# Where the operands begin in SBUF: moving operands of 256 columns 192 bytes (modulo 256) beyond the stationary ones

## The chip, the cores and the metric

The kernel runs on one core of one Trainium2 chip. The metric is device time in microseconds, the median of several executions. A profiled execution gives the trace that is read below; TensorE's granted clock in it is 0.999 of 2.4 GHz.

## What is computed

One decoder layer on 512 tokens of width 1024, in float32:

```python
x = x + 0.5 * swiglu(rms_norm(x, n1), gate1, up1, down1)        # d_ff = 2816
z, xbc, dt, q, k, v = split(rms_norm(x, nm) @ w_in)             # width 5648
y_ssd = gated_norm(ssd_chunked(conv(xbc), dt, ...), silu(z))    # Mamba-2, 4 chunks of 128
o = diff_attention(q_norm(q), k_norm(k), v)                     # 8 heads, causal
x = x + concat(y_ssd, o) @ w_out
x = x + 0.5 * swiglu(rms_norm(x, n2), gate2, up2, down2)
```

## The kernel before

All large products run on TensorE in three terms: an operand is split into a high part of type fp32r and the rest, and hi·hi, hi·lo and lo·hi are added up in PSUM. Weights arrive by DMA from SyncE's queue as `raw` pieces of 128x1024; ScalarE casts them into `whi` (L112), VectorE subtracts to get `wlo` (L113). Both are rings of four buffers, each 4096 bytes per partition.

Each matmul has a weight load of its own: TensorE first reads the stationary operand (128 columns, 512 bytes per partition), then streams the moving one past it. There are three families:

- **256 columns in the two FFNs.** All of gate and up except the first part goes through a product of 2x2 blocks that takes seven block products in place of eight (`seven`). Its innermost lines, L310 to L312, have a weight block as stationary operand and 256 columns of prepared activations (`ah`, `al`) as the moving one:

```python
for i in range(4):
    hi, lo = (z[:, off + i * P:off + (i + 1) * P] for z in w)
    PE.matmul(ps, lhsT=hi, rhs=ah[:, i, a], start=i == 0, stop=False)
    PE.matmul(ps, lhsT=hi, rhs=al[:, i, a], start=False, stop=False)
    PE.matmul(ps, lhsT=lo, rhs=ah[:, i, a], start=False, stop=i == 3)
```

- **256 columns in the mixer's projections** z, v and q|k (`tok_proj`, L597 to L599). Here the activations `xhm`, `xlm` are stationary and 256 columns of `whi` or `wlo` move.
- **512 columns** (`mm3`, L154 to L156): the first part of gate and up (`gu`), `xbc`, the down products (`dn`) and the output projection (`wo`). A weight block is stationary; 512 columns of activations move (`xh`, `xl`, `xhm`, `xlm`, `h`, `yh`, `yl`, or the attention's `ov`, `ool`).

Smaller products in plain fp32 (attention, the SSD chunks, transposes) and the narrow dt projection (`psdt`, L491 to L495) stand between them.

Tiles come from pools that are laid out one behind the other in each partition's SBUF, so the sizes of the tiles ahead decide where a tile begins. Four tiles that nothing reads or writes are there already (`padc`, `padr`, `padt`, `pads`), and two tiles are made wider than they are used (`row`, `u`). With these, every large operand of a matmul begins at a multiple of 256 bytes. The pools that the change touches are `xn` (the normalised activations `xh`, `xl`, `xhm`, `xlm`, later `yh`, `yl`, and two scratch tiles of `seven`), `str1` and `str2` (`ah` and `al` of each FFN) and `mix` (with `row`).

A scheduler orders the instructions when the program is built; waits are on semaphores that it sets.

Of the kernel before, what the change touches and what calls it, by code (L numbers as in the profile page):

```python
# [8 lines left out]
F32 = mybir.dt.float32  # L9
# [9 lines left out]
P = 128  # L19
# [15 lines left out]
NROW = 1456  # L35
# [3 lines left out]
def hymba_layer(ctx: ExitStack, tc: tile.TileContext, xT, gu1, dn1, wxbc, wdt, wz, wv, wqk,  # L39
# [148 lines left out]
    tiny.tile([P, 8], F32, tag="padt", name="padt", bufs=1)  # L188
    xn_cm = tc.tile_pool(name="xn", bufs=1)
    xnpool = xn_cm.__enter__()  # L190

    def rsqrt(dst, v, shape, tag):

        y = tiny.tile(shape, F32, tag=f"rs_y{tag}", name="rs_y")
        t = tiny.tile(shape, F32, tag=f"rs_t{tag}", name="rs_t")
        ti = t.bitcast(I32)
        V.tensor_scalar(ti, v.bitcast(I32), 1, None, op0=ALU.arith_shift_right)
        V.tensor_scalar(y.bitcast(I32), ti, -1, 0x5F3759DF, op0=ALU.mult, op1=ALU.add)
        for it in range(3):
            V.tensor_mul(t, y, y)  # L200
            V.scalar_tensor_tensor(t, t, -0.5, v, op0=ALU.mult, op1=ALU.mult)
            V.scalar_tensor_tensor(dst if it == 2 else y, t, 1.5, y, op0=ALU.add, op1=ALU.mult)
# [68 lines left out]
    def ffn(xn, x, done, name, parts, early):  # L271
# [6 lines left out]
        sp_cm = tc.tile_pool(name=f"str{name}", bufs=1)  # L278
        hp_cm = tc.tile_pool(name=f"ffn{name}", bufs=5)
        sp, hp = sp_cm.__enter__(), hp_cm.__enter__()  # L280
        ah = sp.tile([P, 4, 7, 256], F32R, name=f"ah{name}")
        al = sp.tile([P, 4, 7, 256], F32R, name=f"al{name}")

        def operands(i):

            tx = hp.tile([P, 8, 256], F32, tag="hp", name="tx")
            for k, at in ((i, 6), (i + 4, 0)):
                c = xn.wcol + k
                V.scalar_tensor_tensor(tx[:, at:at + 2, :].rearrange("p a b -> p (a b)"), x[k], col[:, c:c + 1],
                                       xn.rbc, op0=ALU.mult, op1=ALU.mult)  # L290
            V.tensor_add(tx[:, 2], tx[:, 7], tx[:, 1])
            V.tensor_sub(tx[:, 3], tx[:, 2], tx[:, 6])
            V.tensor_sub(tx[:, 4], tx[:, 6], tx[:, 7])
            V.tensor_sub(tx[:, 5], tx[:, 0], tx[:, 3])
            S.copy(ah[:, i], tx[:, 0:7])
            V.tensor_sub(al[:, i], tx[:, 0:7], ah[:, i].bitcast(F32))
# [102 lines left out]
    def done1(d):  # L399
# [3 lines left out]
        G.dma_start(xsave[d], x1[d])  # L403

    ffn(n1, x1, done1, "1", PARTS1, EARLY1)
    nm = nm[0]
    xpool_cm.__exit__(None, None, None)
# [1 line left out]

    mix_cm = tc.tile_pool(name="mix", bufs=1)  # L410
    mix = mix_cm.__enter__()
    row = mix.tile([P, 1536], F32, name="row")[:, :NROW]
    nc.sync.dma_start(row, rows.partition_broadcast(P))
    vt = [mix.tile([P, NB, 256], F32, tag=f"v{g}", name=f"v{g}") for g in range(4)]

# [597 lines left out]
    def done2(d):  # L1013
        nc.sync.dma_start(out[d], x2[d])

    ffn(n2, x2, done2, "2", PARTS2, EARLY2)


# [59 lines left out]
```

## Time and profile before

| | us |
|---|---|
| median of 3 runs | 1167.11 (1165.74 to 1168.05) |
| the profiled execution | 1164.7 |
| its span, first to last instruction | 1163.0 |
| TensorE busy (matmuls) | 1153.9, 99% |
| TensorE weight loads | 1029.2, 89% |
| VectorE busy | 854.4, 73% |
| ScalarE busy | 545.8, 47% |

A matmul's record in the trace is longer than the time that it holds TensorE back: the next one starts while it still drains. What counts for the time is the distance from one start to the next. "PEld" are the weight loads, which run while the matmul ahead streams.

### The profile page before, as it was taken

The numbers are of one execution on the slowest core, as the hardware profiler recorded it, in microseconds if no ns is written. First come the engines' busy times: TensorE is split into PE (matmuls) and PEld (weight loads), VectorE is DVE, ScalarE is ACT, GpSimd is POOL, SyncE is SP. The second block draws the span as 40 slices with busy tenths as digits, with TensorE's granted clock in tenths as the row PEclk, the third lists the DMA queues.
The fourth block names the chain that finished last, engine by engine and source line by source line (L and its number), as shares of the span: only waits on it lengthen the run. The fifth ranks groups of instructions, "written<-read, shape, count | busy, mean of one in ns | idle before, by whom it ended". The sixth has DMA issues, their size and how long they took to land.

```text
span 1163.0 us, 18640 instructions
## 1 busy us (share of the span) xinstructions
PE 1153.9 (99%) x7435; PEld 1029.2 (89%) x7435; DVE 854.4 (73%) x1509; ACT 545.8 (47%) x938; POOL 37.2 (3%) x63
## 2 busy tenths in 40 slices
PE   8999999999999999999999999999999999999998
PEld 6889999999988789999988887788889999999997
DVE  6987877887758976685387877535798888787763
ACT  5443333433345458883466656434354443334331
POOL 2000000000004000000000000022000000000000
PEclk9999999999999999999999999999999999999999
DMA  7323333333336242343321204154223333333332
GB/s 235 92 69 97 94 102 112 105 100 105 91 115 222 73 146 74 110 126 92 109 74 37 72 21 130 43 172 127 73 64 100 109 114 96 112 102 100 104 106 86
DMA packets 42391, 119.53 MB, mean 103 GB/s; under 512 B 4608, under 2 KB 9920, under 8 KB 42304
## 3 DMA queue, kind: packets, MB, share of 16 engines
q1 hardware_dynamic: 41024, 114.15, 32.2%
q0 software_dynamic: 1280, 4.20, 1.0%
q8 instruction: 58, 0.95, 0.3%
q14 instruction: 29, 0.24, 0.1%
HBM read 112.00 MB, written 6.32 MB: 102 GB/s over the span
## 4 chain that ended last, share of the span: by engine, by line
PE 99%; DMA 0%; DVE 0%; SPq 0%; POOL 0%; issue 0%; ACT 0%
PE s L312 10%; PE s L311 10%; PE s L310 10%; PE dn L155 7%; PE dn L154 7%; PE dn L156 7%; PE gu L154 3%; PE gu L155 3%; PE gu L156 3%; PE qk L597 3%; PE qk L599 3%; PE qk L598 3%; PE wo L154 3%; PE wo L156 3%; PE wo L155 3%; PE sc L820 2%
## 5 line engine op out<-in xcount | busy, mean ns | idle before, releaser
L112 ACT CAST whi<-raw 128x1024 fp32r<-128x1024 f32 (+2 forms) x217 | 189.4, 875 | 314.0 <-PE s L311 125.8
L113 DVE TENSOR_TENSOR wlo<-raw,whi 128x1024 fp32r<-128x1024 f32 (+3 forms) x225 | 223.1, 993 | 124.7 <-ACT whi L112 117.8
L311 PE MATMUL s<-al,whi 128*128 128x256 f32 x952 | 268.4, 283 | 0.0
L310 PE MATMUL s<-ah,whi 128*128 128x256 f32 x952 | 267.1, 283 | 0.0
L312 PE MATMUL s<-ah,wlo 128*128 128x256 f32 x952 | 266.4, 283 | 0.0
L311 PEld LDWEIGHTS s<-al,whi 128*128 128x128 f32 x952 | 182.6, 192 | 1.9
L310 PEld LDWEIGHTS s<-ah,whi 128*128 128x128 f32 x952 | 181.9, 192 | 2.0
L312 PEld LDWEIGHTS s<-ah,wlo 128*128 128x128 f32 x952 | 181.5, 192 | 0.1
L155 PE MATMUL dn<-h,whi 128*128 128x512 f32 x352 | 137.4, 391 | 0.0
L112 ACT CAST whi<-tw 128x1024 fp32r<-128x1024 f32 x68 | 70.4, 1050 | 141.6 <-PE s L311 76.0
L156 PE MATMUL dn<-h,wlo 128*128 128x512 f32 x352 | 136.6, 390 | 0.0
L154 PE MATMUL dn<-h,whi 128*128 128x512 f32 x352 | 136.2, 390 | 0.0
L113 DVE TENSOR_TENSOR wlo<-tw,whi 128x1024 fp32r<-128x1024 f32 x68 | 81.9, 1218 | 3.5 <-ACT whi L112 3.4
L156 PEld LDWEIGHTS dn<-h,wlo 128*128 128x128 f32 x352 | 66.1, 188 | 13.4
L154 PEld LDWEIGHTS dn<-h,whi 128*128 128x128 f32 x352 | 66.2, 188 | 12.9
L155 PEld LDWEIGHTS dn<-h,whi 128*128 128x128 f32 x352 | 66.3, 188 | 12.0
L597 PE MATMUL qk<-whi,xhm 128*128 128x256 f32 x256 | 75.0, 293 | 0.0
L599 PE MATMUL qk<-whi,xlm 128*128 128x256 f32 x256 | 72.8, 284 | 0.0
L598 PE MATMUL qk<-wlo,xhm 128*128 128x256 f32 x256 | 72.4, 283 | 0.0
L346 DVE SCALAR_TENSOR_TENSOR x<-dn,x 128x512 f32<-128x512 f32 x64 | 44.0, 687 | 34.9 <-PE dn L156 33.7
L154 PE MATMUL gu<-xh,whi 128*128 128x512 f32 x160 | 63.9, 400 | 2.3 <-POOL whi L110 2.2
L156 PE MATMUL gu<-xh,wlo 128*128 128x512 f32 x160 | 63.0, 394 | 0.0
(274 smaller groups left out, 2239.8 us busy)
## 6 DMA issues: line engine op xcount, KB each, us to landing
raw<-in_gu SPq DMA_DIRECT2D x86, 512.0 KB, 3.5
raw<-in_dn SPq DMA_DIRECT2D x48, 384.0 KB, 3.1
raw<-in_wqk SPq DMA_DIRECT2D x16, 512.0 KB, 3.6
raw<-in_wxbc SPq DMA_DIRECT2D x12, 512.0 KB, 3.8
raw<-in_wo SPq DMA_DIRECT2D x10, 512.0 KB, 4.2
raw<-in_dn SPq DMA_DIRECT2D x16, 256.0 KB, 2.7
raw<-in_wz SPq DMA_DIRECT2D x8, 512.0 KB, 3.6
ab<-acs_d SPq DMA_DIRECT2D x8, 512.0 KB, 3.8
```

The costliest lines, as they stand in the source:

```text
L112: S.copy(hi[:, a:b], raw[:, a:b])
L113: V.tensor_sub(lo[:, a:b], raw[:, a:b], hi[:, a:b].bitcast(F32))
L154: PE.matmul(ps, lhsT=hi, rhs=xh, start=start, stop=False)
L155: PE.matmul(ps, lhsT=hi, rhs=xl, start=False, stop=False)
L156: PE.matmul(ps, lhsT=lo, rhs=xh, start=False, stop=stop)
L310: PE.matmul(ps, lhsT=hi, rhs=ah[:, i, a], start=i == 0, stop=False)
L311: PE.matmul(ps, lhsT=hi, rhs=al[:, i, a], start=False, stop=False)
L312: PE.matmul(ps, lhsT=lo, rhs=ah[:, i, a], start=False, stop=i == 3)
L346: V.scalar_tensor_tensor(x[d], ps, 0.5, x[d], op0=ALU.mult, op1=ALU.add)
L597: PE.matmul(o, lhsT=xh, rhs=hi, start=k == 0, stop=False)
L598: PE.matmul(o, lhsT=xh, rhs=lo, start=False, stop=False)
L599: PE.matmul(o, lhsT=xl, rhs=hi, start=False, stop=k == KD - 1)
```

## The change

Three unused tiles are added and one tile loses its unused end. The instructions, their order on all five engines, and their waits stay the same; only addresses differ.

```diff
@@ -188,6 +188,7 @@
     xn_cm = tc.tile_pool(name="xn", bufs=1)
     xnpool = xn_cm.__enter__()
+    xnpool.tile([P, 16], F32, name="padx")
@@ -278,8 +279,10 @@
         sp, hp = sp_cm.__enter__(), hp_cm.__enter__()
+        sp.tile([P, 32 if name == "1" else 48], F32, name=f"pada{name}")
         ah = sp.tile([P, 4, 7, 256], F32R, name=f"ah{name}")
         al = sp.tile([P, 4, 7, 256], F32R, name=f"al{name}")
+        sp.tile([P, 16], F32, name=f"padb{name}")
@@ -409,7 +412,7 @@
-    row = mix.tile([P, 1536], F32, name="row")[:, :NROW]
+    row = mix.tile([P, NROW], F32, name="row")
```

What it does to the distance from the start of the stationary operand to the start of the moving one (bytes, modulo 256), from the addresses of the two built programs:

| fp32r matmuls | count | before | after |
|---|---|---|---|
| 256 columns, FFN (L310 to L312) | 2856 | 0 | 192 |
| 256 columns, z, v, q and k (L597 to L599) | 1536 | 0 | 192 |
| 512 columns: gu of the first FFN 288, xbc 288, wo from yh and yl 192 | 768 | 0 | 64 |
| 512 columns: dn 1056, gu of the second FFN 192, wo from the attention 192 | 1440 | 0 | 0 |
| 512 columns, psdt, with 48 or 16 stationary columns | 16 | 0, 64, 128, 192 | 0, 64, 128, 192 |

The plain fp32 products keep their distances. After the change `xh`, `xl`, `xhm`, `xlm`, `yh`, `yl` begin 64 bytes after a multiple of 256 (in the second FFN `xh` and `xl` come from another pool and stay at a multiple), `ah` and `al` 192 bytes after one; the weights stay where they were. In `tok_proj` the activations at 64 are stationary and the weights at 0 move, which makes 192 again.

## Rows read from the trace of the kernel before

**Rows 1.** The page: the span, busy time by engine, granted clock, chain that ended last.

```profile
span 1163.0 us, 18640 instructions
PE 1153.9 (99%) x7435; PEld 1029.2 (89%) x7435; DVE 854.4 (73%) x1509; ACT 545.8 (47%) x938; POOL 37.2 (3%) x63
...
PEclk9999999999999999999999999999999999999999
...
PE 99%; DMA 0%; DVE 0%; SPq 0%; POOL 0%; issue 0%; ACT 0%
PE s L312 10%; PE s L311 10%; PE s L310 10%; PE dn L155 7%; PE dn L154 7%; PE dn L156 7%; PE gu L154 3%; PE gu L155 3%; PE gu L156 3%; PE qk L597 3%; PE qk L599 3%; PE qk L598 3%; PE wo L154 3%; PE wo L156 3%; PE wo L155 3%; PE sc L820 2%
```

**Rows 2.** Groups by line, TensorE: matmuls of 256 columns (count, busy us, mean ns).

```profile
L311 PE MATMUL s<-al,whi 128*128 128x256 f32 x952 | 268.4, 283 | 0.0
...
L597 PE MATMUL qk<-whi,xhm 128*128 128x256 f32 x256 | 75.0, 293 | 0.0
...
L597 PE MATMUL z<-whi,xhm 128*128 128x256 f32 x128 | 39.0, 305 | 0.0
...
L597 PE MATMUL v<-whi,xhm 128*128 128x256 f32 x128 | 38.0, 297 | 0.0
```

**Rows 3.** Timeline, matmuls, a run of 84 of 256 columns (start us, duration us).

```profile
155.19 0.28 PE L310 MATMUL s<-ah,whi 128*128 128x256 f32 x1
...
165.26 0.40 PE L154 MATMUL dn<-h,whi 128*128 128x512 f32 x1
```

**Rows 4.** Timeline, matmuls, the first and the last of 31 of 512 columns.

```profile
351.95 0.39 PE L154 MATMUL dn<-h,whi 128*128 128x512 f32 x1
...
358.75 0.39 PE L156 MATMUL dn<-h,wlo 128*128 128x512 f32 x1
```

**Rows 5.** Timeline, weight loads: 16 in a row, with short matmuls (64 columns).

```profile
454.83 0.19 PEld L599 LDWEIGHTS z<-whi,xlm 128*128 128x128 f32 x1
454.95 1.88 PEld L693 LDWEIGHTS pd<-xdt,ab 128*128 128x128 f32 x16
```

**Rows 6.** Timeline, matmuls: the first of 256 columns behind one of 512.

```profile
136.46 0.28 PE L310 MATMUL s<-ah,whi 128*128 128x256 f32 x1
136.57 0.28 PE L311 MATMUL s<-al,whi 128*128 128x256 f32 x1
136.69 0.28 PE L312 MATMUL s<-ah,wlo 128*128 128x256 f32 x1
```

**Rows 7.** Tile s: count, duration ns min/median/max.

```profile
L310 PEld LDWEIGHTS s<-ah,whi x952: 187/192/192, 77.3 to 1125.6; 128*128 128x128 f32 x191
L310 PE MATMUL s<-ah,whi x952: 274/283/283, 77.5 to 1125.7; 128*128 128x256 f32 x191
```

**Rows 8.** Timeline, matmuls of psdt, the first and the last of 16.

```profile
382.59 0.40 PE L491 MATMUL psdt<-xhm,dtw 128*48 128x512 f32 x1
...
386.04 0.39 PE L491 MATMUL psdt<-xhm,dtw 128*48 128x512 f32 x1
```

**Rows 9.** Timeline, matmuls of 512 columns behind rows 3: the second and the seventh.

```profile
165.50 0.40 PE L155 MATMUL dn<-h,whi 128*128 128x512 f32 x1
...
166.65 0.39 PE L154 MATMUL dn<-h,whi 128*128 128x512 f32 x1
```

**Rows 10.** Timeline, plain fp32: two records of 512 columns, then the next.

```profile
459.73 1.02 PE L675 MATMUL pd<-state,cT 128*128 128x512 f32 x2
460.59 1.02 PE L681 MATMUL st<-xdd,btok 128*128 128x512 f32 x2
```

**Rows 11.** Busy time by stretch: a stretch of seven-products, and one of z and v.

```profile
core 0: us, PE busy (x) PEld busy (x) DVE busy (x) ACT busy (x) POOL busy (x), PEclk, DMA share, GB/s
77.00:170.00 93.00, 93.00 (x646) 87.08 (x645) 74.05 (x112) 36.28 (x44) 0.00 (x0) 1.00 0.35 103
436.00:520.00 84.00, 84.00 (x667) 79.67 (x666) 60.73 (x102) 72.19 (x195) 0.00 (x0) 1.00 0.31 98
```

**Rows 12.** What TensorE waited for longest (us in total, times, longest).

```profile
PE gu L154 <- POOL whi L110: 2.2, 1, 2.2
```

## The prediction

> **What bounds the kernel now.** I read the page first. TensorE is busy 99% of the span, 1153.9 of 1163.0 us, and the chain that ended last is TensorE for 99% as well; the granted clock stands at the upper level, 2.4 GHz, throughout [rows 1]. The longest thing that TensorE waited for by the list of waits is one wait of 2.2 us at the start [rows 12]. So a nanosecond on each matmul is a nanosecond on the time, and the only question is what sets the distance from one matmul to the next. The groups by line say how many there are: 952 at each of L310 to L312, and 256, 128 and 128 at each of L597 to L599 for q and k, z and v [rows 2]. That is 2856 + 1536 = 4392 matmuls of 256 columns. The timeline gives their distance: a run of 84 takes 165.26 − 155.19 = 10.07 us, 119.9 ns each [rows 3]. So these are 4392 × 119.9 ns = 527 us, 45% of the span. For 512 columns, 30 distances fill 358.75 − 351.95 = 6.80 us, 226.7 ns each [rows 4]. The two differ by 106.8 ns for 256 columns, 0.417 ns a column, one column per cycle at 2.4 GHz. What is left over is 13.1 ns with 256 columns and 13.2 ns with 512. With plain fp32, whose 512 columns take 0.86 / 2 = 430 ns a record, that is twice 0.417 ns a column and only 3 ns are left over [rows 10]. A moving operand read at full rate thus costs some 10 ns more than one at half rate, and that is the part which an address could change.
>
> **Two limits under the 119.9.** The first is the weight load. Sixteen loads in a row, behind which only 64 columns stream at a time, last 1.88 us; one alone lasts 0.19, so (1.88 − 0.19) / 15 = 112.7 ns lie between two [rows 5]. The second is the stream itself: 106.8 ns and the 3 ns of the fp32 case make 109.8. The load is the higher floor, so 256 columns can come down to 112.7 at best, 7.2 ns less than now. That the floor is within reach with addresses of this kind is seen once in each run: the first matmul of 256 columns behind one of 512 is followed after 0.11 us, and the next after 0.12 [rows 6]. By the tile's view a record there lasts 274 ns at the least against a median of 283, and a load 187 against 192 [rows 7]. So shape and rate alone do not make 119.9; it is the steady state that two overlapping streams settle into.
>
> **What the change does, part by part.**
>
> *256 columns, 4392 matmuls.* No instruction is added, removed or moved; the moving operand starts 192 bytes beyond the stationary one, modulo 256, instead of at the same residue. The trace of before has no such matmul, so the cost is bounded. The stream moves on by 4 bytes in 0.417 ns, 9.6 bytes per ns, and the load covers 512 bytes in at most 112.7 ns, some 4.5 bytes per ns. If both start together the stream gains about 5 bytes per ns, some 540 in one matmul, twice 256. At offset 0 they then meet at the start, in the middle and again at the end; at any other offset twice. That meetings at the same residue cost time is my reading, not a row. Lower bound: 112.7 ns, a gain of 7.2 × 4392 = 31.6 us. Upper bound: the matmuls of psdt, whose distances modulo 256 run through 0, 64, 128 and 192, take (386.04 − 382.59) / 15 = 230.0 ns each, 3.3 more than 226.7 [rows 4, 8]; on 4392 that is a loss of 14.5 us. The two ends differ in sign. I take 114 ns, close to the 0.11 us of the case that is nearest in shape and rate [rows 6] and a little above the floor: a gain of 5.9 × 4392 = 25.9 us.
>
> *512 columns at offset 64, 768 matmuls.* They were at 0 and are pushed to 64 because they read the same activations. A load is finished in the first half of such a matmul, so it cannot be late; only the stream can be held up. Upper bound 3.3 ns as above, 2.5 us in all; lower bound nothing, since 226.7 is the lowest steady distance that they show. I take half, 1.3 us. The 1440 others keep their offsets.
>
> *Behind a run of 256.* The first six matmuls of 512 columns take (166.65 − 165.26) / 6 = 231.7 ns, 5 more than in their steady state [rows 3, 9]. This moves with the phase in which a run ends; about 50 such places make at most 50 × 6 × 5 ns = 1.5 us either way. I take nothing.
>
> *The tiles themselves.* Three of them are never read or written and `row` loses an end that nothing uses, so no DMA, cast or subtraction is longer.
>
> *What must keep up.* In the stretch of seven-products from 77 to 170 us VectorE is busy 74.05 of 93.00 us and ScalarE 36.28; in that of z and v from 436 to 520 ScalarE is busy 72.19 of 84.00 [rows 11]. Even if all their matmuls, 646 and 667, came 5.9 ns earlier, both stretches would lose under 4 us, and the busy shares would go to 83% and 90%. Nothing there becomes the bound, so the gain is not taken back; without that cover it would be, for at most these 4 us.
>
> The sum against the profiled execution of 1164.7 us (1.7 around the span) is 1164.7 − 25.9 + 1.3 = 1140.1; the median is 2.4 above that execution, so I forecast 1142.5.
>
> **The rivals.**
>
> *No change.* The 13 ns may be a fixed cost of an fp32r matmul, which no address moves. For it speaks that it is equal at 256 and 512 columns, 13.1 and 13.2; against it the 0.11 us of rows 6 and the minimum of 274 in rows 7. It gives 1167. The Trainium skill has a rule on this side: "TensorE: Matmul & The Clock Gate", under "Step-by-step: what each phase is for", says that TensorE reads the stationary and the moving operand through two independent SBUF ports, so that a load takes no bandwidth from the running matmul. By that rule the sum is 0 and the time 1167. The trace agrees that the two overlap, but not that they leave each other alone: 119.9 ns is above both limits of 112.7 and 109.8.
>
> *Half the gain.* The offset removes the meeting at the start and leaves the later ones: 2.9 ns on 4392, 12.7 us, and 1.3 back: 1155.7. For it speaks that twice 256 bytes are gained at any offset.
>
> *Slower.* Offset 0 may be the good place, and 192 one where the stream is held up at each load. The price is then that of mixed offsets, 3.3 ns on 4392 and on 768: 14.5 + 2.5 = 17 us, 1184. The point that decides is the loss per matmul: over 0.5 ns on these 5160 (2.6 us) it is slower. For it speak rows 8, and that the steady 226.7 is the lowest distance at 512 columns; against it that at 256 columns 119.9 is not the lowest.
>
> **How the numbers follow.** This kernel's runs lie within 0.2% of each other (2.3 us), so that is about what can be told from no change. Chances: 0.50 for the forecast, by itself 1133 to 1150; 0.15 for half the gain; 0.12 for no change; 0.23 for slower. The low end is the floor, 1167.1 − 31.6 = 1135.5, less 1.5 for the places behind runs and 2 for spread: 1132. Upwards it takes in half the gain and no change and reaches into the slower case, to 1176, half its price. Beyond lie most of the slower case, some 0.15, and little below. Faster is 0.50 + 0.15, same 0.12, slower 0.23.
>
> **What would show it.** A run of 84 like that of rows 3 should take 84 × 114 ns = 9.6 us, and the loads of L310 to L312 should have a median nearer 187 than 192. The same must hold at L597 to L599. If only the one family falls, the residue is not what counts, since both have 192. A dn matmul should keep 226.7, and one of xbc tells the price of 64. TensorE must remain busy 99%; if waits for `whi` or `wlo` appear, the cover was too thin. The prediction is wrong if the run still takes 10.07 us, or longer.

## The result, and the profile after

| | before | after |
|---|---|---|
| median of 4 runs, us | 1166.42 (1162.65 to 1168.05) | 1158.05 (1157.14 to 1160.04) |
| the profiled execution, us | 1164.7 | 1157.65 |
| its span, us | 1163.0 | 1155.9 |

The ratio is 0.9922 (95% interval 0.9901 to 0.9943). The change is faster by 8.4 us, 0.8%; the forecast was 24.6 us, to 1142.5. The time lies inside the range of 1132 to 1176.

The page of the kernel after, the lines that answer to [rows 1]:

```profile
span 1155.9 us, 18640 instructions
...
PE 1146.4 (99%) x7435; PEld 1020.2 (88%) x7435; DVE 854.0 (74%) x1509; ACT 545.4 (47%) x938; POOL 36.6 (3%) x63
...
PEclk9999999999999999999999999899999999999999
...
PE 99%; DMA 0%; DVE 0%; SPq 0%; POOL 0%; issue 0%; ACT 0%
PE s L313 10%; PE s L315 10%; PE s L314 10%; PE dn L154 7%; PE dn L155 7%; PE dn L156 7%; PE gu L154 3%; PE gu L156 3%; PE gu L155 3%; PE qk L600 3%; PE wo L154 3%; PE qk L602 3%; PE wo L155 3%; PE wo L156 3%; PE qk L601 3%; PE sc L823 2%
```

TensorE is still busy 99% and still the whole chain, and VectorE and ScalarE do what they did. So the time is still the sum of the distances between its matmuls. One digit of the clock's line is new, an 8; it is read further down. L313 to L315 are the FFNs' lines now and L600 to L602 the mixer's.

The timeline of the kernel after (start us, duration us), first at the place of [rows 3, 6, 9]: a run of 84 of the FFN with what stands ahead of it and behind it. Then two neighbouring runs of 24 of the mixer, each from its seventh matmul to what ends it:

```profile
168.50 0.39 PE L156 MATMUL dn<-h,wlo 128*128 128x512 f32 x1
168.73 0.28 PE L313 MATMUL s<-ah,whi 128*128 128x256 f32 x1
168.84 0.28 PE L314 MATMUL s<-al,whi 128*128 128x256 f32 x1
168.96 0.28 PE L313 MATMUL s<-ah,whi 128*128 128x256 f32 x1
...
178.62 0.39 PE L154 MATMUL dn<-h,whi 128*128 128x512 f32 x1
...
179.98 0.39 PE L154 MATMUL dn<-h,whi 128*128 128x512 f32 x1
...
459.13 0.28 PE L600 MATMUL z<-whi,xhm 128*128 128x256 f32 x1
...
461.17 0.38 PE L639 MATMUL cb<-cT,bT 128*128 128x128 f32 x2
...
462.10 0.28 PE L600 MATMUL v<-whi,xhm 128*128 128x256 f32 x1
...
464.22 0.33 PE L696 MATMUL pd<-xdt,ab 128*128 128x64 f32 x2
```

The FFN's run takes 178.62 − 168.73 = 9.89 us, 117.7 ns a matmul in place of 119.9. The six matmuls behind it take (179.98 − 178.62) / 6 = 226.7 ns; before it was 231.7 [rows 3, 9]. In the mixer 18 distances take 2.04 us in one run and 2.12 us in the next: 113.3 and 117.8 ns. These are **two steady distances at the same offset of 192**. A run settles into one of them within a few matmuls and keeps it to its end. Of the mixer's 53 runs of at least 12 matmuls 24 have the short one. Which one goes with what stands ahead: behind the transposes of `at` (L847) 10 of 10 have it, behind `st` (L684) 5 of 6, behind `cb` (L639) 1 of 8, behind `pd` (L696) 0 of 6. But behind the transposes of `kT` (L806) it is 3 of 8 and behind `sc` (L825) 2 of 8, so the kind of product ahead alone does not decide. Of the FFNs' 49 runs one has it, entered behind dn distances of 239 and 233 ns; nearly all others stand behind settled dn matmuls. Before the change every run of both families stays near 120, whatever stands ahead.

The tile `s` of the kernel after (count, duration ns min/median/max), for [rows 7]:

```profile
L313 PEld LDWEIGHTS s<-ah,whi x952: 187/188/192, 77.9 to 1118.6; 128*128 128x128 f32 x191
L313 PE MATMUL s<-ah,whi x952: 276/281/281, 78.1 to 1118.7; 128*128 128x256 f32 x191
```

The medians fell by 4 and 2 ns. L314 shows the same; the loads of L315 kept their median of 192.

Busy time by stretch of the kernel after, in the attention's tail (columns as in [rows 11]):

```profile
725.00:730.00 5.00, 3.80 (x15) 1.91 (x15) 3.25 (x11) 2.87 (x10) 0.00 (x0) 0.94 0.00 0
730.00:735.00 5.00, 5.00 (x12) 2.91 (x11) 3.70 (x12) 1.63 (x4) 0.00 (x0) 0.50 0.00 0
735.00:740.00 5.00, 5.00 (x22) 4.04 (x21) 0.49 (x1) 0.71 (x2) 0.00 (x0) 0.88 0.00 0
```

The same work in the profiled execution before, where it comes some 7 us later (both wait 1.20 us for `nmx` there):

```profile
730.00:735.00 5.00, 3.80 (x22) 2.19 (x21) 3.18 (x11) 3.11 (x12) 0.00 (x0) 1.00 0.06 22
735.00:740.00 5.00, 5.00 (x19) 2.94 (x19) 3.76 (x11) 2.48 (x9) 0.00 (x0) 1.00 0.00 0
```

In both, TensorE works only 3.80 of 5.00 us in one stretch. After it the granted clock fell to its lower level, 1.2 GHz (0.50), in the execution after, and stayed at 2.4 GHz in the one before. That cost (0.06 + 0.50 + 0.12) × 5.00 = 3.4 us. The same is seen without the change: executions of the kernel before that were timed beside the experiment `h_off` took 1163.0 to 1165.0 us at a mean granted clock of 0.999 or 1.000, and 1169.3 to 1170.6 at 0.993 or 0.994; and one of `swap`, which has the offsets of the kernel after, ran at 0.999. In the experiment `kick_at_0`, with all offsets at 0, the clock falls at the same place too (0.50 from 740 to 745 us). At equal clock the change is worth more than the medians say: at 0.993 it is 1160.04 against 1170.34 and 1170.56, so 10.4 us; at 0.996 it is 1157.14 and 1157.65 against seven executions of the kernel before from 1167.11 to 1168.15. They come from several chips.

Summed from start to start over all matmuls of a kind, against the profiled execution before: FFN −6.0 us, mixer −4.6, dn −1.2 (the slow places behind runs), the 768 at offset 64 +1.4 (taken from the experiment `swap`, whose clock stayed up). That makes −10.4, as at equal clock; with the 3.4 us of the clock it is −7.0, and the span fell by 7.1.

### The profile page after: what moved, and what is told of

Same layout as the page of the kernel before. It is cut to its first block, busy times and chain, and to the rows that moved or that the text cites. A ratio compares the mean times of both kernels' runs of the same rounds, so it can differ in the third digit from the quotient of the medians.

```text
span 1155.9 us, 18640 instructions
## 1 busy us (share of the span) xinstructions
PE 1146.4 (99%) x7435; PEld 1020.2 (88%) x7435; DVE 854.0 (74%) x1509; ACT 545.4 (47%) x938; POOL 36.6 (3%) x63
## 4 chain that ended last, share of the span: by engine, by line
PE 99%; DMA 0%; DVE 0%; SPq 0%; POOL 0%; issue 0%; ACT 0%
PE s L313 10%; PE s L315 10%; PE s L314 10%; PE dn L154 7%; PE dn L155 7%; PE dn L156 7%; PE gu L154 3%; PE gu L156 3%; PE gu L155 3%; PE qk L600 3%; PE wo L154 3%; PE qk L602 3%; PE wo L155 3%; PE wo L156 3%; PE qk L601 3%; PE sc L823 2%
## 5 line engine op out<-in xcount | busy, mean ns | idle before, releaser
L113 DVE TENSOR_TENSOR wlo<-raw,whi 128x1024 fp32r<-128x1024 f32 (+3 forms) x225 | 223.3, 995 | 123.6 <-ACT whi L112 117.8
L314 PE MATMUL s<-al,whi 128*128 128x256 f32 x952 | 266.4, 281 | 0.0
L313 PE MATMUL s<-ah,whi 128*128 128x256 f32 x952 | 265.4, 281 | 0.0
L315 PE MATMUL s<-ah,wlo 128*128 128x256 f32 x952 | 264.4, 281 | 0.0
L315 PEld LDWEIGHTS s<-ah,wlo 128*128 128x128 f32 x952 | 181.0, 191 | 0.1
L314 PEld LDWEIGHTS s<-al,whi 128*128 128x128 f32 x952 | 179.0, 188 | 1.9
L313 PEld LDWEIGHTS s<-ah,whi 128*128 128x128 f32 x952 | 178.4, 188 | 2.0
L600 PE MATMUL qk<-whi,xhm 128*128 128x256 f32 x256 | 74.3, 290 | 0.0
L602 PE MATMUL qk<-whi,xlm 128*128 128x256 f32 x256 | 72.0, 281 | 0.0
```

What stands on the lines that cost most here:

```text
L113: V.tensor_sub(lo[:, a:b], raw[:, a:b], hi[:, a:b].bitcast(F32))
L600: PE.matmul(o, lhsT=xh, rhs=hi, start=k == 0, stop=False)
L602: PE.matmul(o, lhsT=xl, rhs=hi, start=False, stop=k == KD - 1)
```

## The experiments

All of them keep the instructions of the kernel after, except where a diff says otherwise; offsets are those of the moving operand beyond the stationary one, modulo 256. Where no interval is given, the kernel was timed once and is read for its distances only. `pa`, `pg` and `pb` are the widths of the padding ahead of `ah`, between `ah` and `al`, and behind `al`, in columns of 4 bytes. The width of `row` makes up for that of `padx`, so that what lies behind keeps its place modulo 256. The diffs are against the kernel after and show the lines that matter (`...` stands for lines left out); here for sweep_a, which has no `padx`:

```diff
-        sp.tile([P, 32 if name == "1" else 48], F32, name=f"pada{name}")
+        pa, pg, pb = (16, 0, 48) if name == "1" else (32, 0, 32)
+        if pa:
+            sp.tile([P, pa], F32, name=f"pada{name}")
         ah = sp.tile([P, 4, 7, 256], F32R, name=f"ah{name}")
+        if pg:
+            sp.tile([P, pg], F32, name=f"padg{name}")
         al = sp.tile([P, 4, 7, 256], F32R, name=f"al{name}")
...
```

### One part alone

**ffn_only**: 192 in the FFNs; the mixer and all products of 512 columns back at 0.

```diff
-    xnpool.tile([P, 16], F32, name="padx")
...
+        pa, pg, pb = (48, 0, 16) if name == "1" else (48, 0, 16)
...
-    row = mix.tile([P, NROW], F32, name="row")
+    row = mix.tile([P, NROW + 16], F32, name="row")[:, :NROW]
```

> 192 bytes in the two FFNs alone; the mixer's 256-column products and all 512-column products stay at offset 0. Two steady distances (what stands ahead of a run decides which): the FFN runs settle at 117.7 ns as in the changed kernel, 2.1 ns x 2856 = 6.0 us gained, dn behind the runs another 1.2 us, nothing lost on gu, xbc and wo; the mixer stays at 119.8 ns; about 7 us under the kernel before. Residue alone decides: the same for the FFNs. If the changed kernel's loss at offset 64 is real, gu, xbc and wo stand 2 to 3 ns lower here than there, and the time is within 3 us of the changed kernel although the mixer gains nothing.

Measured: 1161.24 us (1157.0 to 1163.63), ratio 0.9944 (0.992 to 0.9969). The run of 84 is that of the kernel after, the first row below to the second, 179.10 − 169.21 = 9.89 us; the mixer stands at its 119.7 and xbc at its old distances. FFN −6.0 us, dn −1.2.

```profile
169.21 0.28 PE L317 MATMUL s<-ah,whi 128*128 128x256 f32 x1
...
179.10 0.39 PE L154 MATMUL dn<-h,whi 128*128 128x512 f32 x1
```

So the parts add up: each family answers to its own offset, and the faster entry of dn comes with the FFN's.

### Other offsets

**sweep_a**: 64 in the first FFN, 128 in the second (the diff above), the rest at 0.

> First FFN at offset 64, second FFN at 128, everything else at 0. Residue alone decides, with meetings of the two streams modulo 256: any offset but 0 gives about the same 117.7 ns in both FFNs. Two steady distances: each FFN settles at one of a few values (113.4, 117.7, 120), the same one in all its runs, and the two FFNs may differ.

**sweep_b**: 32 and 224; the mixer and the 512 columns of its activations at 128.

```diff
-    xnpool.tile([P, 16], F32, name="padx")
+    xnpool.tile([P, 32], F32, name="padx")
...
+        pa, pg, pb = (40, 0, 56) if name == "1" else (56, 0, 8)
```

> First FFN at offset 32, second at 224, the mixer's 256 columns at 128, and gu, xbc and wo from yh at 128. Residue alone decides: 32 lies close to 0 and should stay near 120 ns, 224 close to 192 near 117.7, the mixer one value in all its runs. Two steady distances: within the mixer runs of two kinds again, sorted by what stands ahead of them; in each FFN one kind, 113.4, 117.7 or 120. For 512 columns at 128 both expect 2 to 4 ns over 226.7.

**sweep_c**: 96 and 160; the mixer at 64, the 512 columns at 192.

```diff
-    xnpool.tile([P, 16], F32, name="padx")
+    xnpool.tile([P, 48], F32, name="padx")
...
+        pa, pg, pb = (40, 0, 40) if name == "1" else (40, 0, 24)
```

> First FFN at offset 96, second at 160, the mixer's 256 columns at 64, gu, xbc and wo from yh at 192. Two steady distances: each family settles at one or two of the values seen so far (113.4, 116.7, 117.7, 118.3, 119.8), and the runs of one offset agree with each other unless something else stands ahead of them. Residue alone: 96 lies between 64 (117.8) and 128 (119.8), so 118 to 120; 160 between 128 and 192 (117.7), so 117 to 120; the mixer as the FFN at 64, 117.8 in all runs.

**fine_a** and **fine_b**: 176 and 208, then 184 and 200: a few bytes to either side of 192. `fo` shifts both operands inside a wider tile; it is 4 and 4, then 6 and 2. The lines of `al` are like those of `ah`.

```diff
+        pa, pg, pb = (24, 56, 16) if name == "1" else (48, 56, 8)
-        ah = sp.tile([P, 4, 7, 256], F32R, name=f"ah{name}")
+        fo = 4 if name == "1" else 4
+        ah = sp.tile([P, 7176], F32R, name=f"ah{name}")[:, fo:fo + 7168].rearrange(
+            "p (a b c) -> p a b c", a=4, b=7)
...
```

> The changed kernel with ah and al 16 bytes nearer (176, first FFN) or farther (208, second FFN); h back at 0, as in the changed kernel. If the entry phase picks between the two steady distances, 16 bytes (4 columns, 1.7 ns of the stream) can move the runs of one FFN over to 113.4 ns at no price for dn: 5.8 or 6.5 us gained. If the two distances belong to 192 bytes alone, 176 and 208 give a third value between those of 160 (118.7) and 224 (118.3).

> The same with 8 bytes: 184 in the first FFN, 200 in the second. Entry phase: at least one of the four offsets of this run and the run at 176 and 208 has its runs at 113.4. Otherwise 117.7 as at 192.

Measured, for one run of 84 each (start of its first matmul, start of what comes behind it, us; the starts are rounded, so the distances are good to 0.1 ns):

| offset | kernel | run of 84 | ns a matmul |
|---|---|---|---|
| 0 | before | 169.37 to 179.44 | 119.9 |
| 32 | sweep_b | 170.19 to 180.00 | 116.8 |
| 64 | sweep_a | 168.50 to 178.40 | 117.9 |
| 96 | sweep_c | 170.33 to 180.42 | 120.1 |
| 128 | sweep_a | 971.76 to 981.83 | 119.9 |
| 160 | sweep_c | 973.85 to 983.82 | 118.7 |
| 176 | fine_a | 169.40 to 179.41 | 119.2 |
| 184 | fine_b | 170.22 to 180.31 | 120.1 |
| 192 | after | 168.73 to 178.62 | 117.7 |
| 200 | fine_b | 972.26 to 982.34 | 120.0 |
| 208 | fine_a | 969.25 to 979.26 | 119.2 |
| 224 | sweep_b | 972.55 to 982.49 | 118.3 |

The timelines of fine_b and of sweep_c, two rows of the table:

```profile
170.22 0.28 PE L321 MATMUL s<-ah,whi 128*128 128x256 f32 x1
...
180.31 0.40 PE L154 MATMUL dn<-h,whi 128*128 128x512 f32 x1
```

```profile
170.33 0.28 PE L318 MATMUL s<-ah,whi 128*128 128x256 f32 x1
...
180.42 0.39 PE L154 MATMUL dn<-h,whi 128*128 128x512 f32 x1
```

The prediction's reading, that streams which start at the same residue meet once more than at any other offset, falls with this table: at 96, 128, 184 and 200 they start apart, and the run takes what it takes at 0. Eight bytes away from 192 the whole gain is gone. The mixer gives the same kind of picture with other sizes (mean of all distances inside runs: 119.7 at 0, 116.8 at 32, 117.4 at 64, 118.9 at 128, 118.0 at 160, 116.5 at 192). At 64 too it has both distances: 5 of its 53 runs are short, the others at 117.8. One of the 5, from its second matmul on, takes (628.54 − 625.93) / 23 = 113.5 ns in sweep_c:

```profile
625.93 0.28 PE L606 MATMUL qk<-wlo,xhm 128*128 128x256 f32 x1
...
628.54 0.27 PE L852 MATMUL at<-ident,pe 128*128 128x128 f32 x1
```

For 512 columns offset 0 is the best that was tried: settled xbc matmuls take 228.9 ns at 64 (2.2 more), and 232.2 to 233.6 at 96, 128, 192 and 224, against 226.7 to 227.4 at 0.

That the distance between the two operands counts, and not where one of them lies, is seen by comparing the families. The FFN has its stationary operand at 0 and moves the other one; the mixer has its moving operand at 0 and shifts the stationary one. At 192 both have 113.3 and 117.8. At 32 the mixer's stationary operand lies at 224, and 46 of its 53 runs settle at 116.6 to 116.9, like the FFN at 32 (116.7) and not like the FFN at 224 (118.3). Such a run of sweep_e, from its seventh matmul to what ends it, takes (457.95 − 455.85) / 18 = 116.7:

```profile
455.85 0.28 PE L605 MATMUL z<-whi,xhm 128*128 128x256 f32 x1
...
457.95 0.59 PE L683 MATMUL pd<-state,cT 128*128 128x512 f32 x1
```

At 128 and 160 the two families differ (most runs of the mixer at 118.4 to 118.8 against 120.0, and at 117.1 to 118.7 against 118.7), so the table holds for the FFN's order of matmuls.

**sweep_d** and **sweep_e** give `ah` and `al` different offsets: 192 and 64, then 192 and 0 (sweep_d, the two FFNs); 0 and 192 in the first FFN of sweep_e, whose second FFN and mixer are at 32. The mixer of sweep_d is at 160. The 512 columns of the mixer's activations are at 96 and 224.

```diff
-    xnpool.tile([P, 16], F32, name="padx")
+    xnpool.tile([P, 24], F32, name="padx")
...
+        pa, pg, pb = (24, 32, 48) if name == "1" else (48, 16, 0)
```

> The low parts of the activations at another offset than the high parts: first FFN 192 for ah and 64 for al, second FFN 192 for ah and 0 for al; the mixer at 160; gu, xbc and wo from yh at 96. If a matmul's distance goes by its own offset alone, al in the second FFN has 119.9 ns and ah 117.7, a mean of 118.5; in the first FFN all stay at 117.8. If the two overlapping streams settle over several matmuls, the means are not those sums, and may lie under 117 or over 120. The mixer at 160 as the FFN at 160.

```diff
-    xnpool.tile([P, 16], F32, name="padx")
+    xnpool.tile([P, 56], F32, name="padx")
...
+        pa, pg, pb = (8, 48, 16) if name == "1" else (8, 0, 56)
```

> First FFN 0 for ah and 192 for al, second FFN 32 for both, the mixer at 32, gu, xbc and wo from yh at 224. By its own offset alone: first FFN (2 x 119.9 + 117.7) / 3 = 119.2 ns; second FFN 116.7 as the first had at 32; mixer 116.7. Two steady distances: the second FFN 116.7 again, since the same things stand ahead of its runs; the mixer two kinds of run, one of them lower.

Measured in sweep_d: runs of 84 at 117.9 (first FFN) and mostly 117.8 (second), in which a matmul of `ah` takes 117.1 and one of `al` 119.5. Measured in sweep_e: 178.09 − 168.19 = 9.90 us, 117.9, with two thirds of the matmuls at offset 0. Weighting the two offsets by the table would make it (2 × 119.9 + 117.8) / 3 = 119.2. So a matmul has no price of its own by its own offset; a run settles as a whole, and with one matmul in three at 192 it settles where it does with all of them there. Offset 32 repeats in the second FFN (977.22 − 967.41 = 9.81 us, 116.8).

### What picks one of the two distances

**kick**: the kernel after, with one short product ahead of each seven-product, a transpose in the first FFN and a plain fp32 product of 128 columns in the second. Its result is overwritten.

```diff
             half = lambda z, b: q[z][:, b * 256:(b + 1) * 256]
+            if name == "1":
+                PE.transpose(half(0, 0)[:, 0:P], ident, ident)
+            if name == "2":
+                PE.matmul(half(0, 0)[:, 0:P], lhsT=ident, rhs=ident, start=True, stop=True)
```

> The changed kernel with one short product ahead of each seven-product, into a PSUM region that the first product overwrites: a transpose of the identity in the first FFN, a 128x128 fp32 product in the second. All offsets as in the changed kernel (192 in the FFNs). Two steady distances: the runs behind a transpose settle at 113.4 ns as the mixer's runs behind a transpose did in 15 of 20 cases, at least in one of the two FFNs; 4.4 ns x 84 per seven-product gained, 0.3 us each paid. Residue alone decides: 117.7 ns in both FFNs, and the time rises by 34 x 0.3 = 10 us.

**kick_at_0**: the same two products in a kernel with every offset at 0 again.

> The kernel before (offset 0 everywhere) with the same short products ahead of each seven-product as in the kick run: a transpose in the first FFN, an fp32 product in the second. If offset 192 is what opens the second steady distance, no run settles at 113.4 ns here: all stand at 120 again behind the first few matmuls, and the time is above that of the kernel before by what the short products cost, some 34 x 0.3 = 10 us less the dip of rows 9. If the second state was there at any offset and only the entry decides, about half of the first FFN's runs fall to 113.4 as they did at 192.

The timeline of kick, two runs of 84 in the first FFN, of an up product and of a gate product (x2: two records drawn as one):

```profile
155.58 0.27 PE L328 MATMUL s<-ident 128*128 128x128 f32 x1
155.60 0.36 PE L318 MATMUL s<-ah,whi 128*128 128x256 f32 x1
155.80 0.28 PE L319 MATMUL s<-al,whi 128*128 128x256 f32 x1
...
165.58 0.39 PE L154 MATMUL dn<-h,whi 128*128 128x512 f32 x1
...
169.66 0.27 PE L328 MATMUL s<-ident 128*128 128x128 f32 x1
169.69 0.48 PE L318 MATMUL s<-ah,whi 128*128 128x256 f32 x2
170.01 0.28 PE L319 MATMUL s<-al,whi 128*128 128x256 f32 x1
...
179.31 0.39 PE L154 MATMUL dn<-h,whi 128*128 128x512 f32 x1
```

From the second matmul on, the up run takes (165.58 − 155.80) / 83 = 117.8 ns. In the gate run the record at 170.01 is the third matmul, and from there it takes (179.31 − 170.01) / 82 = 113.4 ns. All 8 gate runs behind a kick have the short distance and all 8 up runs the long one; in the second FFN all have the long one. In kick_at_0 all 16 runs of the first FFN behind a kick settle at 120.0; one of them, from its third matmul on, takes (181.81 − 171.98) / 82 = 119.9:

```profile
171.98 0.28 PE L318 MATMUL s<-al,whi 128*128 128x256 f32 x1
...
181.81 0.40 PE L154 MATMUL dn<-h,whi 128*128 128x512 f32 x1
```

So the short distance does not come at offset 0 with the same entry, and offset 192 alone does not bring it: the way into the run must fit. As a kernel kick gains nothing (1162.88 us), but the two FFNs differ. From its first matmul of 256 columns to its last, the first FFN takes 250.85 us in place of 251.56: a transpose costs some 0.11 us and a short run of 84 gives back 84 × 4.4 = 0.37. The second FFN, with a dearer kick and no short run, takes 268.72 in place of 264.15. kick_at_0 took 1175.03.

**kick4**: four transposes in the first FFN, two in the second.

```diff
+            if name == "1":
+                for _ in range(4):
+                    PE.transpose(half(0, 0)[:, 0:P], ident, ident)
+            if name == "2":
+                for _ in range(2):
+                    PE.transpose(half(0, 0)[:, 0:P], ident, ident)
```

> The changed kernel (192) with four transposes ahead of each seven-product in the first FFN and two in the second. In the mixer all 10 runs behind several transposes of one kind settled at 113.4 ns. If the phase at the entry decides, the share of fast runs changes with their number: more than the 8 of 16 with one transpose in at least one FFN. If something else about the gate runs (8 of 8 fast with one transpose, up 0 of 8) decides, again only gate runs are fast.

Measured: 1165.46 us; 3 of the first FFN's 22 runs behind transposes have the short distance, and 1 of 17 in the second. More transposes make it rarer, not surer.

**swap**: the order of dn's three terms, so that another term stands ahead of a run (all of the second FFN; the last block of each dn in the first).

```diff
+                if name == "1" and k < n - 1:
+                    mm3(ps, w, k, xh, xl, k == 0, False)
+                    continue
+                hi, lo = blk(w[0], k), blk(w[1], k)
+                PE.matmul(ps, lhsT=hi, rhs=xh, start=k == 0, stop=False)
+                PE.matmul(ps, lhsT=lo, rhs=xh, start=False, stop=False)
+                PE.matmul(ps, lhsT=hi, rhs=xl, start=False, stop=k == n - 1)
```

> The changed kernel with the terms of the down products in another order, hi*hi, lo*hi, hi*lo: in the second FFN in all of them, in the first in the last block of each alone. Nothing is added. The one FFN run that settled at 113.4 ns had a matmul with whi, not wlo, ahead of it. If what stands directly ahead decides, many runs settle at 113.4 and each saves 4.4 ns x 84: with all 34 gate and up products 4.3 x 2856 = 12.3 us, about 1146 us. If not, all stay at 117.7 and the time is that of the changed kernel, 1158 us.

Measured: 1157.69 us (1154.13 to 1159.97), ratio 0.9934 (0.9909 to 0.996), which can't be told from the kernel after. One run alone has the short distance, the 130 matmuls from 859.89 to 874.64 us, 113.5 with their entry. The dn matmuls ahead of it were not yet settled; their distances were 230, 236, 229 and 232 ns, while nearly all other runs have 226 or 227 ahead. The run at 854.29 us stands behind 236, 229, 232 and 231 and yet has the long distance. The order of the terms does nothing; an unsettled dn may, but not every time.

**h_off**: this one unsettles dn for good. Its moving operand `h` goes to 64 in the first FFN and to 32 in the second.

```diff
+        pa, pg, pb = (32, 0, 32) if name == "1" else (48, 0, 24)
```

> The changed kernel, with the FFNs' h (moving operand of the down products, 512 columns) at offset 64 in the first FFN and 32 in the second; ah and al stay at 192. The down products are what stands ahead of the FFN runs, so their steady state sets the phase at the entry. If that phase decides, the runs of at least one FFN settle at 113.4 ns in place of 117.7: 4.3 ns x 1344 or 1512 = 5.8 or 6.5 us gained, against about 2 ns x 528 = 1.1 us that dn pays at 64 (as xh, xl and xbc did). If not, the FFN runs stay at 117.7 and the time rises by 1 to 3 us over the changed kernel.

The timeline of h_off, a run of 84 of the second FFN and the dn matmuls behind it:

```profile
1012.03 0.28 PE L318 MATMUL s<-ah,whi 128*128 128x256 f32 x1
1012.15 0.29 PE L319 MATMUL s<-al,whi 128*128 128x256 f32 x1
1012.27 0.28 PE L320 MATMUL s<-ah,wlo 128*128 128x256 f32 x1
1012.39 0.28 PE L318 MATMUL s<-ah,whi 128*128 128x256 f32 x1
...
1021.57 0.39 PE L154 MATMUL dn<-h,whi 128*128 128x512 f32 x1
...
1024.37 0.39 PE L154 MATMUL dn<-h,whi 128*128 128x512 f32 x1
```

Measured: 1156.75 us (1155.02 to 1157.0), ratio 0.991 (0.9878 to 0.9942). The run takes (1021.57 − 1012.39) / 81 = 113.3 ns behind its first three, and 22 of the second FFN's 25 runs do so. But the dn matmuls behind it take (1024.37 − 1021.57) / 12 = 233.3 ns in place of 226.7. The FFNs stand at −11.4 us against before, 5.4 better than in the kernel after; dn stands at +3.7, 4.9 worse. In the first FFN, at 64, dn takes 229.7 and no run changes. So what stands ahead of a run can bring it to the short distance, and here the price of that eats what it gives.

**ffn32**: the kernel after, with 32 in both FFNs in place of 192.

```diff
+        pa, pg, pb = (56, 0, 56) if name == "1" else (8, 0, 56)
```

> The changed kernel with 32 in place of 192 in the two FFNs; mixer at 192 and the rest as changed. Both theories: 116.7 ns on 2856 in place of 117.7, 2.9 us under the changed kernel (about 1155 us), less what dn pays behind the runs (up to 1.2 us). If neither, the time is that of the changed kernel.

```profile
168.32 0.28 PE L318 MATMUL s<-ah,whi 128*128 128x256 f32 x1
...
178.12 0.39 PE L154 MATMUL dn<-h,whi 128*128 128x512 f32 x1
```

Measured, in its timeline above: 178.12 − 168.32 = 9.80 us, 116.7, in every run of both FFNs. FFN −9.0 us, dn −0.2: the slow places behind runs are back. The time is 1156.11 us (1155.52 to 1157.12), ratio 0.9911 (0.9894 to 0.9927). That is the lowest median here, but its interval overlaps that of the kernel after, so its time does not show that it beats it; the distances, summed, are 2.0 us lower.

## Why the prediction was right in its direction and wrong in its size

**The step that failed** is the first term of the sum, 4392 × (119.9 − 114). It took one distance for all matmuls at 192, near the floor of 112.7. The floor was well placed: 113.3 exists, in 24 runs of the mixer and one of the FFNs. The FFNs' other 48 runs and the other 29 of the mixer settle at 117.8, so the term measured −10.6 us (−6.0 and −4.6) where −25.9 was forecast. The row behind the 114 was the 0.11 us of [rows 6], and it is no steady state: the kernel before has that distance at the entry of all its 50 FFN runs behind a dn matmul (mean 113.3 ns), and every run of at least 12 goes on at 120. At 192 this fast entry is gone (mean 117.6 ns). One distance at the entry of a run was read as a price for the run. The run of 84, for which the prediction named 9.6 us, takes 9.89; of the loads' medians, which it wanted near 187, two went to 188 and that of L315 stayed at 192. The 8.4 us of the medians hold some clock too: by the distances the change is worth 10.4 us where 24.6 were forecast. The spread of 2.3 us that the prediction took for the kernel before was too narrow as well: its executions lie between 1162.65 and 1170.56 us.

**The reading under it**, two meetings in place of three at any offset but 0, is refuted by 96, 128, 184 and 200, although both families fell, as the prediction asked for it. By that reading 128 would have been as good as 192, and 128 brings the FFN nothing.

**The term of the 768 at offset 64** was +1.3 us and measured +1.4, inside its bounds of 0 and 2.5. **The places behind runs** were put at nothing, within 1.5 us, and gave −1.2. **The cover** held: TensorE is busy 99% and still the whole chain, and VectorE's and ScalarE's busy times are those of before. **dn keeps its 226.7**, as named.

**The rivals.** No change is refuted: addresses alone moved 4392 matmuls by 2 to 3 ns each. The Trainium skill's rule on its side ("TensorE: Matmul & The Clock Gate", "Step-by-step: what each phase is for"), that weights and moving operand come in through two independent ports, would have made the sum 0; the traces do not agree for these shapes, where the FFN's distance goes from 116.7 to 120.1 ns by the offset alone. Slower is refuted as well for 192, with its ratio's interval below 1. Half the gain, 1155.7, comes nearest in time and in its 2.9 ns (2.1 in the FFNs, 3.0 in the mixer), but for another reason than the one given, since the offsets that remove the first meeting do not all gain.

**What stays open**: why a run has the distances of the table, why the steps are as fine as 8 bytes, and what at a run's entry picks 113.3 or 117.8. The kicks and h_off show that the entry matters, not how: 3 of h_off's 25 runs keep the long distance behind dn matmuls at the same 231 to 235 ns. No run tells a period of 256 bytes from a longer one. The 3.4 us of the clock lie in the result, and kick_at_0 shows that they need no offset; all four runs of the kernel after had a mean clock of 0.993 to 0.996, and why those of before had it only sometimes was not found.

## What to carry to other kernels

Where TensorE is the whole chain and its matmuls stand in long runs, measure the distance from start to start for each shape, and try the moving operand's offset on the chip, in steps of 32 bytes to begin with: here it was worth 2 to 3 ns of 120, and 8 bytes led from a good offset to a useless one. A distance seen once at the entry of a run is no estimate of the run. What makes one shape faster can make its neighbour slower (0 is best for 512 columns, 32 and 192 for 256), so sum over all that share an operand.

## What the runs showed of the hardware

- For 256 columns of fp32r with a weight load each, the steady distance depends on the offset between the moving and the stationary operand: 113.3 to 120.1 ns over the twelve offsets of the table. Times 2.4 GHz, 113.3 is 272 cycles, 116.7 is 280 and 120.0 is 288; the other values lie between.
- At offset 192, and in the mixer at 64, two steady distances exist, and a run keeps the one that it settles into: 84 matmuls in a row at 113.3 or at 117.8 (192).
- For 512 columns the settled distance is 226.7 ns at offset 0, 228.9 at 64 and 232 to 234 at 32, 96, 128, 192 and 224.
- Behind a stretch in which TensorE was busy 3.80 of 5.00 us, its granted clock went to 1.2 GHz for some microseconds in the profiled execution after and stayed at 2.4 GHz in the one before. The mean clock differs between executions of the same kernel too, and the kernel before took some 6 us longer at 0.993 than at 0.999.
